# A gather, running-sum and matmul kernel: undivided gathers and stores, a shorter lead of the sums and single casts

## The chip, the cores and the metric

The kernel runs on one core of a Trainium2 chip. The metric is the device time of one execution in microseconds (us). An execution's span, from the first to the last instruction that the hardware profiler recorded, is a little shorter than its time.

## The reference

```python
B, S, N, D = (16, 4096, 2048, 512)
# x: [B, S, D] float32; indices: [B, N], sorted, without repeats; w: [D, D] float32
def reference(x, indices, w):
    b_idx = np.arange(B)[:, None]
    gathered = x[b_idx, indices, :].copy()      # 2048 rows of 2 KB for each batch
    cs = np.cumsum(gathered, axis=1)            # running sum over the gathered rows
    return np.matmul(cs, w).astype(np.float32)  # [B, N, D]
```

67.1 MB are gathered from memory and 67.1 MB are written back.

## The kernel before, in words

**Tiles.** The 16 x 2048 gathered rows are cut into T = 256 tiles of 128 rows (P = 128), 16 tiles for each batch (NT = 16). Two tiles make a pair (R = 2), so there are G = 128 pairs. Every tile goes through the same six steps, and each step is written out for one engine. There is no scheduler: every engine has its own list of instructions, and waits on semaphores (through the helper class `Lane`, whose `need` leaves out a wait already made).

1. **Gather (POOL, L138-164).** An indirect DMA fetches 128 rows of x by index into the float32 buffer `g32`, one row for each partition. There are 16 tile slots in `g32` (NG = 16, eight pairs). A pair's gathers wait until the casts of the pair that used the slots before are done (`pool.need(s_c, ...)`, L141).
2. **Cast (ACT, L169-179).** `g32` to the half-precision buffer `g16` (NH = 8 pairs). A cast waits for its gather's 16 semaphore increments, one from each DMA engine.
3. **Sums (PE, L181-196).** Four 128x128 matmuls against a triangular matrix give the running sums inside the tile, transposed, in one of four PSUM tiles `pa` (NA = 4).
4. **Carry (DVE, L198-223).** Adds the last column of the previous tile and writes `cst` (NC = 4 pairs).
5. **Product (PE, L225-240).** Four 128x512 matmuls by w into one of four PSUM tiles `pb` (NB = 4).
6. **Drain (ACT, L242-245) and store (SP, L247-267).** `pb` is copied to the output buffer `ob` (NO = 4 buffers of W = 2 pairs), and SP issues a DMA to the output: 512 KB for one pair, 1 MB for two.

**What sets the order.** On PE the list `order` (L378-386) puts the sums of tile u + LEAD ahead of the product of tile u. LEAD is 3 in the steady state; it grows from 1 at the start and shrinks to 1 at the end. On ACT the list `casts` (L125-133) says which casts stand ahead of the drain of tile u: far = 6 tiles ahead in the steady state, 2 to 5 at the start, and 5 to 3 over the last tiles. Where far is over 5 the two tiles of a pair are cast by one instruction of 128x1024; where it is smaller each tile has its own 128x512 cast. The steady states of PE, DVE and ACT are hardware loops; ACT's holds V = 3 x 16 = 48 tiles.

**Divided transfers.** Five gathers (`SPLITS`: tiles 56, 104, 152, 200 and 248) are issued in two parts. First an instruction resets the cursor of the descriptor generator (L152), then the last E = 8 partitions are gathered with an index list of their own (`idx_last`, semaphore `s_h`), and then the other 120. One store is issued in two parts as well: that of pair `ODD` = 106 and the pair after it, 1 MB, goes out as partitions 0 to 118 (`EVEN` = 119) and partitions 119 to 127 (L264-267, semaphore `s_x`).

**Stores.** The first eight pairs are stored one at a time, then two pairs per DMA, and the last two pairs one at a time (L293-298). The very first and the very last pair are stored tile by tile (L254-260).

Of the kernel before, what the change touches and what calls it, by code (L numbers as in the profile page):

```python
# [7 lines left out]
P = 128  # L8
FP32 = mybir.dt.float32
FP16 = mybir.dt.float16  # L10
U32 = mybir.dt.uint32
# [22 lines left out]
def kernel(  # L34
# [7 lines left out]
    nc = tc.nc  # L42

    B, S, D = x.shape
    N = indices.shape[1]
    R = 2
    Q = P // R
    DC = D // P
    NT = N // P
    T = B * NT  # L50
    G = T // R
    GB = NT // R
    KI = T // P
    E = 8
    EB = 3
    SPLITS = [b * NT + NT // 2 for b in range(EB, B, EB)]
    ODD = G - 11 * R
    EVEN = 119
    FIRST = 2 * R
    NG = 16  # L60
    LEAD = 3
    FAR = 6
    NH = 8
    NA = 4
    NB = 4
    NC = 4
    W = 2
    NO = 4
    U = NT
    V = EB * U  # L70
    assert U == NT == NG == W * R * NO and V % U == 0 and (T - 4 * U) % V == 0 and SPLITS[0] // V == 1 and 2 * U < SPLITS[0] and SPLITS[-1] >= T - 2 * U <= R * ODD + W * R * NO and ODD % W == 0 and U % NG == 0 and U % NA == 0 and U % (R * NC) == 0 and U % NB == 0
# [8 lines left out]
    idx_last = const.tile([E, len(SPLITS), 2], U32)  # L80
# [10 lines left out]
    g32 = [const.tile([P, R, D], FP32, name=f"g32_{i}") for i in range(NG // R)]  # L91
    g16 = [const.tile([P, R, D], FP16, name=f"g16_{i}") for i in range(NH)]
# [16 lines left out]
    s_last = sem("s_last")  # L109
    s_h = sem("s_h")  # L110
    s_f = [sem(f"s_f{i}") for i in range(NO)]
    s_x = sem("s_x")
    s_ol = sem("s_ol")
    s_g = [sem(f"s_g{i}") for i in range(NG)]
    s_o = [sem(f"s_o{i}") for i in range(NO)]
# [10 lines left out]
    cast_by = []  # L126
    for u in range(T):
        far = min(FAR, 2 if u < R else 3 + (u + 4) // 8, 3 + (T - 1 - u) // 6)
        casts.append([])
        while len(cast_by) <= min(u + far, T - 1):  # L130
            n = R if far > 5 and len(cast_by) % R == 0 else 1
            casts[u].append((len(cast_by), n))
            cast_by += [cast_by[-1] + 1 if cast_by else 1] * n

    for u in range(2 * U + U, T - 2 * U):
        assert casts[u] == [(t + U, n) for t, n in casts[u - U]]

    def gather(t):  # L138
        g, r = divmod(t, R)
        if t >= NG:  # L140
            pool.need(s_c, cast_by[R * (g + 1) - NG - 1])  # L141
        if t < FIRST:
            pool.need(s_first[g], 16)
            ap = idx_first[:, t, 0:1]
        else:
            pool.need(s_prep, t // P + 1)
            ap = idxg[:, t // P, t % P : t % P + 1]
        parts = [(0, P, ap, s_g[t % NG])]
        if t in SPLITS:

            pool.need(s_last, 16)
            nc.gpsimd.inc_swdge_sem([], [], mode="reset_dge_cursor")  # L152
            parts = [
                (P - E, P, idx_last[:, SPLITS.index(t), 0:1], s_h),
                (0, P - E, ap[: P - E], s_g[t % NG]),
            ]
        for a, b, ap, done in parts:
            nc.gpsimd.indirect_dma_start(  # L158
                out=g32[g % (NG // R)][a:b, r, :],
                out_offset=None,  # L160
                in_=x_flat,
                in_offset=bass.IndirectOffsetOnAxis(ap=ap, axis=0),
                element_offset=(t // NT) * S * D,
            ).then_inc(done, 16 * EB if done is s_h else 16)

    PLAIN = (0, 1, G - 2, G - 1)

    def cast(t, n, first=None):  # L169
        g, r = divmod(t, R)  # L170
        for u in range(t, t + n):
            act.need(s_g[u % NG], 16 * (u // NG + 1), first)
            if first is None and u in SPLITS:
                act.need(s_h, 16 * EB * (SPLITS.index(u) + 1))
            elif first is not None and u == SPLITS[0] - 2 * U:
                act.need(s_h, 16 * EB - 2 * U, first)
        nc.scalar.copy(  # L177
            out=g16[g % NH][:, r : r + n], in_=g32[g % (NG // R)][:, r : r + n]
        ).then_inc(s_c, 1)

    def sums(t, u, first=None):  # L181
        g, r = divmod(t, R)
        tiles = None if first is None else R * first
        pe.need(s_c, cast_by[t] if first is None else cast_by[2 * U + t] - 2 * U // R, first)
# [62 lines left out]
    def store(g, n):  # L247
        b, h = divmod(g, GB)
        rows = out[b, h * R * P : (h + n) * R * P, :]
        i = g // W % NO  # L250
        src = ob[i]

        done = s_ol if g >= G - W else s_f[i] if 0 < g < W * NO and g % W else s_o[i]
# [9 lines left out]
        rows = rows.rearrange(order, p=P, j=R)  # L263
        for part in (slice(0, EVEN), slice(EVEN, P)) if g == ODD else (slice(0, P),):  # L264
            nc.sync.dma_start(out=rows[part], in_=src[part, g % W : g % W + n]).then_inc(
                s_x if part.start else done, 16
            )

    with nc.allow_non_contiguous_dma(reason="a few indices, one per partition"):  # L270
        for k, eng in enumerate((nc.sync, nc.scalar)):
            t = k * R
            eng.dma_start(
                out=idx_first[:, t : t + R, :],
                in_=indices[0, t * P : (t + R) * P]
                .bitcast(U32)
                .rearrange("(t p w) -> p t w", p=P, w=2),
            ).then_inc(s_first[k], 16)
        nc.scalar.dma_start(
            out=idx_last[:],  # L280
            in_=indices[EB:B:EB, (NT // 2 + 1) * P - E : (NT // 2 + 1) * P]
            .bitcast(U32)
            .rearrange("b (p w) -> p b w", w=2),
        ).then_inc(s_last, 16)
    idx_rows = indices.bitcast(U32).rearrange("b (t q) -> (b t) q", q=2 * P)
    for k in range(KI):
        nc.sync.dma_start(
            out=idx64[:, k, :], in_=idx_rows[k * P : (k + 1) * P, :]
# [3 lines left out]
        eng.dma_start(out=w32[:, c, :], in_=w[c * P : (c + 1) * P, :]).then_inc(s_w[c], 16)  # L292
    for g in range(W * NO):  # L293
        store(g, 1)
    for g in range(W * NO, G - W, W):
        store(g, W)
    for g in range(G - W, G):
        store(g, 1)
    for i in range(G // W - NO, G // W - 1):
        sp.need(s_o[i % NO], 16 * (i // NO + 1))  # L300
    sp.need(s_ol, 16 * (R + W - 1))

    nc.gpsimd.memset(ident[:], 1.0).then_inc(s_ut, 1)
# [3 lines left out]
        out=ident[:],  # L308
        in_=ident[:],
# [7 lines left out]
        out=ut[:],  # L317
# [103 lines left out]
    def step(u, first=None):  # L421
        if u % (W * R) == 0:
            i, slot = divmod(u // (W * R), NO)
            if first is None and i == 1:
                act.need(s_f[slot], 16 * (W - 1 + (slot == 0) * (R - 1)))
            act.need(s_o[slot], 16 * i, first)
            if first is None and u == R * ODD + W * R * NO:
                act.need(s_x, 16)
        for t, n in casts[u if first is None else 2 * U + u]:
            cast(t if first is None else t - 2 * U, n, first)  # L430
        drain(u, first)

# [38 lines left out]
```

## Time and profile before

| What | Value |
|---|---|
| time, median of 9 runs | 352.31 us (351.5 to 353.89) |
| time of the profiled execution | 352.95 us |
| its span | 351.2 us |
| granted TensorE clock, mean | 0.987 |
| PE / ACT / POOL / DVE busy | 86 / 74 / 71 / 51% |
| moved by DMA | 135.69 MB, mean 386 GB/s |
| packets of the gathers' queue (q0) and of SP's queue (q1) | 50.1% and 48.0% of 16 DMA engines' span |

A line of the view of instructions by group gives: source line, engine, operation, what it writes and reads, count | busy us, mean ns of one | idle time of the engine just before, and what ended most of it. A line of the view of waits gives: who waited, for whom: us in total, times, longest. The view of a source line ends with the time from a DMA's issue to its landing, which is its last semaphore increment. In the view of stages each row gives the busy time of every engine in one stretch of the span, then the granted clock, the DMA share and GB/s. The trace also holds each transfer's 16 landing increments, one by one, with their times; it does not say which DMA engine sent which.

### The profile page before, as it was taken

The numbers are of one execution on the slowest core, as the hardware profiler recorded it, in microseconds if no ns is written. First come the engines' busy times: TensorE is split into PE (matmuls) and PEld (weight loads), VectorE is DVE, ScalarE is ACT, GpSimd is POOL, SyncE is SP. The second block draws the span as 40 slices with busy tenths as digits, with TensorE's granted clock in tenths as the row PEclk, the third lists the DMA queues.
The fourth block names the chain that finished last, engine by engine and source line by source line (L and its number), as shares of the span: only waits on it lengthen the run. The fifth ranks groups of instructions, "written<-read, shape, count | busy, mean of one in ns | idle before, by whom it ended". The sixth has DMA issues, their size and how long they took to land.

```text
span 351.2 us, 6396 instructions
## 1 busy us (share of the span) xinstructions
PE 301.5 (86%) x2066; PEld 152.2 (43%) x2066; DVE 179.2 (51%) x263; ACT 260.8 (74%) x407; POOL 248.7 (71%) x271
## 2 busy tenths in 40 slices
PE   6797969889899898988989899899898899888990
PEld 2343435434444443543544444444444444434540
DVE  1464636545555464554645555455555555544550
ACT  2686778678787877777968778778687777777980
POOL 6777777777777777777777777777777777777400
PEclk9899999999999999999999999999999999999996
DMA  6899999999999999999999999999999999999994
GB/s 201 265 323 380 384 390 343 406 408 392 403 416 413 419 419 415 404 401 412 387 406 418 418 416 410 395 416 409 418 415 389 412 407 416 338 398 412 416 381 179
DMA packets 40139, 135.69 MB, mean 386 GB/s; under 512 B 6060, under 2 KB 6316, under 8 KB 40128
## 3 DMA queue, kind: packets, MB, share of 16 engines
q0 software_dynamic: 20640, 67.13, 50.1%
q1 hardware_dynamic: 18880, 67.90, 48.0%
q10 hardware_dynamic: 608, 0.53, 0.4%
q8 instruction: 5, 0.08, 0.1%
q14 instruction: 6, 0.05, 0.0%
HBM read 68.42 MB, written 67.11 MB: 386 GB/s over the span
## 4 chain that ended last, share of the span: by engine, by line
POOL 39%; DMA 37%; issue 14%; ACT 5%; PE 2%; POOLq 0%; ACTq 0%; SPq 0%
POOL g L158 39%; DMA g<-in_x_dram,idxg 36%; ACT g L177 5%; PE pb L233 2%; ACT ob L245 1%; DMA idx_first<-in_indices_dram 1%; POOLq L338 0%; PE pa L189 0%; ACTq L26 0%; ACTq L436 0%; SPq L467 0%; SPq L98 0%
## 5 line engine op out<-in xcount | busy, mean ns | idle before, releaser
L158 POOL DMA_INDIRECT g<-in_x_dram,idxg x252 | 238.7, 947 | 76.8 <-issue 67.3
L233 PE MATMUL pb<-w,cst 128*128 128x512 f16 x1024 | 263.9, 381 | 0.7 <-DVE cst L221 0.3
L221 DVE TENSOR_TENSOR cst<-pa,cst 128x512 f16<-128x512 f32 x240 | 166.0, 692 | 140.9 <-PE pa L189 140.7
L177 ACT CAST g<-g 128x1024 f16<-128x1024 f32 (+1 forms) x147 | 137.7, 938 | 72.6 <-DMA g<-in_x_dram,idxg 71.7
L245 ACT COPY ob<-pb 128x512 f32<-128x512 f32 x256 | 138.5, 587 | 4.1 <-PE pb L233 4.1
L189 PE MATMUL pa<-ut,g 128*128 128x128 f16 x992 | 97.2, 221 | 35.9 <-ACT g L177 34.9
L189 PEld LDWEIGHTS pa<-ut,g 128*128 128x128 f16 x992 | 68.8, 98 | 116.4 <-ACT g L177 81.0
L233 PEld LDWEIGHTS pb<-w,cst 128*128 128x128 f16 x1024 | 89.6, 98 | 63.1 <-issue 1.6
L208 DVE CAST cst<-pa 128x512 f16<-128x512 f32 x16 | 11.1, 692 | 14.3 <-PE pa L189 14.3
L344 PE MATMUL pb<-zeros 128*128 128x512 f16 x16 | 5.2, 484 | 1.5 <-DVE zeros L348 1.5
L189 PE MATMUL pa<-uq,g 128*128 128x128 f16 x32 | 3.4, 232 | 2.9 <-ACT g L177 2.7
L158 POOL DMA_INDIRECT g<-in_x_dram,idx_last x5 | 4.5, 895 | 1.5 <-issue 1.5
L158 POOL DMA_INDIRECT g<-in_x_dram,idx_first x4 | 4.0, 998 | 1.6 <-issue 0.9
L189 PEld LDWEIGHTS pa<-uq,g 128*128 128x128 f16 x32 | 2.3, 103 | 5.8 <-issue 3.8
L344 PEld LDWEIGHTS pb<-zeros 128*128 128x128 f16 x16 | 1.9, 122 | 4.0 <-issue 1.9
L417 ACT ACT_TABLE_LOAD x1 | 1.3, 1283 | 3.1 <-issue 3.1
L420 ACT CAST w<-w 128x512 f16<-128x512 f32 x2 | 1.1, 614 | 3.1 <-DMA w<-in_w_dram 3.1
L351 DVE CAST idxf<-idx 128x128 f32<-128x128 uint32 x2 | 0.6, 314 | 3.6 <-DMA idx<-in_indices_dram 3.6
L365 DVE CAST w<-w 128x512 f16<-128x512 f32 x2 | 0.9, 477 | 2.4 <-DMA w<-in_w_dram 2.4
L356 PE MATMUL pb<-ident,idxf 128*128 128x128 f32 x2 | 0.6, 300 | 0.6 <-DVE idxf L351 0.6
L348 DVE MEMSET zeros<- 128x256 uint32 x1 | 0.3, 272 | 1.1 <-SPq L98 1.1
L362 DVE CAST idxg<-pb 128x128 uint32<-128x128 f32 x2 | 0.6, 288 | 0.4 <-PE pb L356 0.4
(12 smaller groups left out, 2.4 us busy)
## 6 DMA issues: line engine op xcount, KB each, us to landing
out_dram<-ob SPq DMA_DIRECT2D x58, 1024.0 KB, 8.8
out_dram<-ob SPq DMA_DIRECT2D x8, 512.0 KB, 6.4
g<-in_x_dram,idxg POOLq DMA_INDIRECT x252, 7.7
out_dram<-ob SPq DMA_DIRECT2D x4, 256.0 KB, 5.2
out_dram<-ob SPq DMA_DIRECT2D x1, 952.0 KB
w<-in_w_dram ACTq DMA_DIRECT2D x2, 256.0 KB, 4.6
w<-in_w_dram SPq DMA_DIRECT2D x2, 256.0 KB, 5.5
idx<-in_indices_dram SPq DMA_DIRECT2D x2, 128.0 KB, 2.9
```

The costliest lines, as they stand in the source:

```text
L158: nc.gpsimd.indirect_dma_start(out=g32[g % (NG // R)][a:b, r, :], out_offset=None, in_=x_flat, in_offset=bass.IndirectOffsetOnAxis(ap=ap, ...
L177: nc.scalar.copy(out=g16[g % NH][:, r : r + n], in_=g32[g % (NG // R)][:, r : r + n]).then_inc(s_c, 1)
L189: mm = nc.tensor.matmul(out=pa[t % NA][:, c], lhsT=g16[g % NH][:, r, c * P : (c + 1) * P], rhs=uq[:] if first is None and g in PLAIN else ...
L208: nc.vector.tensor_copy(out=dst, in_=src).then_inc(s_d, 1)
L221: nc.vector.tensor_tensor(out=dst, in0=src, in1=last, op=mybir.AluOpType.add).then_inc(s_d, 1)
L233: mm = nc.tensor.matmul(out=pb[u % NB][:], lhsT=cst[g % NC][:, c, j, :], rhs=w16[:, c, :], start=(c == 0), stop=(c == DC - 1),)
L245: nc.scalar.copy(out=ob[g // W % NO][:, g % W, j], in_=pb[u % NB][:]).then_inc(s_e, 1)
L344: nc.tensor.matmul(out=pb[NB - 1][:], lhsT=zeros[:, :P], rhs=zeros[:], start=True, stop=True)
L351: nc.vector.tensor_copy(out=idxf[:, k, :], in_=idx64[:, k, 0::2]).then_inc(s_if, 1)
L365: nc.vector.tensor_copy(out=w16[:, c, :], in_=w32[:, c, :]).then_inc(s_wc, 1)
L417: nc.scalar.copy(out=spare[:], in_=zeros[:, :1])
L420: nc.scalar.copy(out=w16[:, c, :], in_=w32[:, c, :]).then_inc(s_wc, 1)
```

## The change

- The five divided gathers and the one divided store become whole: `SPLITS`, `ODD`, `idx_last` with its load, the cursor resets and the semaphores `s_last`, `s_h` and `s_x` go.
- LEAD goes from 3 to 2: the sums run two tiles ahead of the products.
- FAR goes from 6 to 4, and every cast is of one tile; ACT's loop body shrinks from 48 to 16 tiles.
- The last four pairs, instead of the last two, are stored singly. The first eight stay as they were.

```diff
-    E = 8
-    EB = 3
-    SPLITS = [b * NT + NT // 2 for b in range(EB, B, EB)]
-    ODD = G - 11 * R
-    EVEN = 119
-    LEAD = 3
-    FAR = 6
+    LEAD = 2
+    FAR = 4
...
-    V = EB * U
+    V = max(U, W * R * NO)
...
     for u in range(T):
-        far = min(FAR, 2 if u < R else 3 + (u + 4) // 8, 3 + (T - 1 - u) // 6)
-        casts.append([])
-        while len(cast_by) <= min(u + far, T - 1):
-            n = R if far > 5 and len(cast_by) % R == 0 else 1
-            casts[u].append((len(cast_by), n))
-            cast_by += [cast_by[-1] + 1 if cast_by else 1] * n
+        far = 2 if u < R else 3 if u < U // 2 or T - 1 - u < R * R else FAR
+        casts.append(range(done, max(done, min(u + far + 1, T))))
+        done = max(done, min(u + far + 1, T))
...
         if t >= NG:
-            pool.need(s_c, cast_by[R * (g + 1) - NG - 1])
+            pool.need(s_c, R * (g + 1) - NG)
...
-        parts = [(0, P, ap, s_g[t % NG])]
-        if t in SPLITS:
-
-            pool.need(s_last, 16)
-            nc.gpsimd.inc_swdge_sem([], [], mode="reset_dge_cursor")
-            parts = [
-                (P - E, P, idx_last[:, SPLITS.index(t), 0:1], s_h),
-                (0, P - E, ap[: P - E], s_g[t % NG]),
-            ]
-        for a, b, ap, done in parts:
-            nc.gpsimd.indirect_dma_start(
-                out=g32[g % (NG // R)][a:b, r, :],
...
+        nc.gpsimd.indirect_dma_start(
+            out=g32[g % (NG // R)][:, r, :],
...
-    def cast(t, n, first=None):
+    def cast(t, first=None):
         g, r = divmod(t, R)
-        for u in range(t, t + n):
-            act.need(s_g[u % NG], 16 * (u // NG + 1), first)
...
+        act.need(s_g[t % NG], 16 * (t // NG + 1), first)
         nc.scalar.copy(
-            out=g16[g % NH][:, r : r + n], in_=g32[g % (NG // R)][:, r : r + n]
+            out=g16[g % NH][:, r, :], in_=g32[g % (NG // R)][:, r, :]
         ).then_inc(s_c, 1)
...
-        for part in (slice(0, EVEN), slice(EVEN, P)) if g == ODD else (slice(0, P),):
-            nc.sync.dma_start(out=rows[part], in_=src[part, g % W : g % W + n]).then_inc(
-                s_x if part.start else done, 16
-            )
+        nc.sync.dma_start(
+            out=rows.rearrange(order, p=P, j=R), in_=src[:, g % W : g % W + n]
+        ).then_inc(done, 16)
...
-    for g in range(W * NO, G - W, W):
+    for g in range(W * NO, G - 2 * W, W):
         store(g, W)
-    for g in range(G - W, G):
+    for g in range(G - 2 * W, G):
         store(g, 1)
```

More of the change, by code (lines that the diff above doesn't have):

```diff
@@ L69 @@
     U = NT
-    V = EB * U
-    assert U == NT == NG == W * R * NO and V % U == 0 and (T - 4 * U) % V == 0 and SPLITS[0] // V == 1 and 2 * U < SPLITS[0] and SPLITS[-1] >= T - 2 * U <= R * ODD + W * R * NO and ODD % W == 0 and U % NG == 0 and U % NA == 0 and U % (R * NC) == 0 and U % NB == 0
+    V = max(U, W * R * NO)
+    assert U == NT == NG == W * R * NO and V % U == 0 and V % (W * R * NO) == 0 and T % V == 0 and U % NG == 0 and U % NA == 0 and U % (R * NC) == 0 and U % NB == 0
     assert D == 512 and N % (R * P) == 0 and T % P == 0
@@ L79 @@
     idx_first = const.tile([P, FIRST, 2], U32)
-    idx_last = const.tile([E, len(SPLITS), 2], U32)
     idx64 = const.tile([P, KI, 2 * P], U32)
@@ L108 @@
     s_idx = [sem(f"s_idx{k}") for k in range(KI)]
-    s_last = sem("s_last")
-    s_h = sem("s_h")
     s_f = [sem(f"s_f{i}") for i in range(NO)]
-    s_x = sem("s_x")
     s_ol = sem("s_ol")
@@ L125 @@
     casts = []
-    cast_by = []
+    done = 0
     for u in range(T):
-        far = min(FAR, 2 if u < R else 3 + (u + 4) // 8, 3 + (T - 1 - u) // 6)
-        casts.append([])
-        while len(cast_by) <= min(u + far, T - 1):
-            n = R if far > 5 and len(cast_by) % R == 0 else 1
-            casts[u].append((len(cast_by), n))
-            cast_by += [cast_by[-1] + 1 if cast_by else 1] * n
-    for u in range(2 * U + U, T - 2 * U):
-        assert casts[u] == [(t + U, n) for t, n in casts[u - U]]
+        far = 2 if u < R else 3 if u < U // 2 or T - 1 - u < R * R else FAR
+        casts.append(range(done, max(done, min(u + far + 1, T))))
+        done = max(done, min(u + far + 1, T))
+    for u in range(2 * U, T - 2 * U):
+        assert casts[u] == range(u + FAR, u + FAR + 1)
     def gather(t):
@@ L147, in gather @@
             ap = idxg[:, t // P, t % P : t % P + 1]
-        parts = [(0, P, ap, s_g[t % NG])]
-        if t in SPLITS:
-            pool.need(s_last, 16)
-            nc.gpsimd.inc_swdge_sem([], [], mode="reset_dge_cursor")
-            parts = [
-                (P - E, P, idx_last[:, SPLITS.index(t), 0:1], s_h),
-                (0, P - E, ap[: P - E], s_g[t % NG]),
-            ]
-        for a, b, ap, done in parts:
-            nc.gpsimd.indirect_dma_start(
-                out=g32[g % (NG // R)][a:b, r, :],
[L160 to L164, printed above, removed]
+        nc.gpsimd.indirect_dma_start(
+            out=g32[g % (NG // R)][:, r, :],
+            out_offset=None,
+            in_=x_flat,
+            in_offset=bass.IndirectOffsetOnAxis(ap=ap, axis=0),
+            element_offset=(t // NT) * S * D,
+        ).then_inc(s_g[t % NG], 16)
     PLAIN = (0, 1, G - 2, G - 1)
-    def cast(t, n, first=None):
+    def cast(t, first=None):
         g, r = divmod(t, R)
-        for u in range(t, t + n):
-            act.need(s_g[u % NG], 16 * (u // NG + 1), first)
[L173 to L176, printed above, removed]
+        act.need(s_g[t % NG], 16 * (t // NG + 1), first)
         nc.scalar.copy(
-            out=g16[g % NH][:, r : r + n], in_=g32[g % (NG // R)][:, r : r + n]
+            out=g16[g % NH][:, r, :], in_=g32[g % (NG // R)][:, r, :]
         ).then_inc(s_c, 1)
@@ L183, in sums @@
         tiles = None if first is None else R * first
-        pe.need(s_c, cast_by[t] if first is None else cast_by[2 * U + t] - 2 * U // R, first)
+        pe.need(s_c, t + 1, tiles)
         pe.need(s_d, t - NA + 1, tiles)
@@ L251, in store @@
         src = ob[i]
-        done = s_ol if g >= G - W else s_f[i] if 0 < g < W * NO and g % W else s_o[i]
+        done = s_ol if g >= G - 2 * W else s_f[i] if 0 < g < W * NO and g % W else s_o[i]
         if g in (0, G - 1):
@@ L262, in store @@
         order = "(g j p) d -> p g j d" if g in PLAIN else "(g p j) d -> p g j d"
-        rows = rows.rearrange(order, p=P, j=R)
-        for part in (slice(0, EVEN), slice(EVEN, P)) if g == ODD else (slice(0, P),):
-            nc.sync.dma_start(out=rows[part], in_=src[part, g % W : g % W + n]).then_inc(
-                s_x if part.start else done, 16
-            )
+        nc.sync.dma_start(
+            out=rows.rearrange(order, p=P, j=R), in_=src[:, g % W : g % W + n]
+        ).then_inc(done, 16)
     with nc.allow_non_contiguous_dma(reason="a few indices, one per partition"):
@@ L278 @@
             ).then_inc(s_first[k], 16)
[L279 to L284, printed above, removed]
     idx_rows = indices.bitcast(U32).rearrange("b (t q) -> (b t) q", q=2 * P)
@@ L294 @@
         store(g, 1)
-    for g in range(W * NO, G - W, W):
+    for g in range(W * NO, G - 2 * W, W):
         store(g, W)
-    for g in range(G - W, G):
+    for g in range(G - 2 * W, G):
         store(g, 1)
-    for i in range(G // W - NO, G // W - 1):
+    for i in range(G // W - NO, G // W - 2):
         sp.need(s_o[i % NO], 16 * (i // NO + 1))
-    sp.need(s_ol, 16 * (R + W - 1))
+    sp.need(s_ol, 16 * (R + 2 * W - 1))
     nc.gpsimd.memset(ident[:], 1.0).then_inc(s_ut, 1)
@@ L426, in step @@
             act.need(s_o[slot], 16 * i, first)
[L427 to L430, printed above, removed]
+        for t in casts[u if first is None else 2 * U + u]:
+            cast(t if first is None else t - 2 * U, first)
         drain(u, first)
```

## The prediction

> **What bounds the kernel now.** I read four things in this order: the page's slices, the waits, POOL's own timeline, and the time that transfers take to land. In the slices the columns are 40 equal parts of the span.
>
> ```profile
> span 351.2 us, 6396 instructions
> ...
> DMA  6899999999999999999999999999999999999994
> GB/s 201 265 323 380 384 390 343 406 408 392 403 416 413 419 419 415 404 401 412 387 406 418 418 416 410 395 416 409 418 415 389 412 407 416 338 398 412 416 381 179
> ```
>
> The DMA engines are over 90% busy from the third slice to the last but one, and where nothing disturbs them they move 416 to 419 GB/s. That is 419/16 = 26.2 GB/s for one engine, so 16 KB (an engine's eighth rows of one gather) cost it 0.63 us and one 2 KB row 0.08 us. 135.69 MB at 419 GB/s are 324 us; what is above that is the start, the end and the dips. No compute engine is as full (PE 86%, in a loop of 1.09 us a tile; ACT 74%). The waits:
>
> ```profile
> ACT g L177 <- DMA g<-in_x_dram,idxg: 71.7, 94, 2.5
> POOL g L158 <- issue: 69.8, 229, 0.3
> POOL g L158 <- ACT g L177: 9.4, 31, 0.3
> ```
>
> ACT waits for gathers to land. POOL waits for nobody: its longest pause is 0.3 us, the same pause that stands ahead of each gather. So it issues one gather every 1.25 us, as its timeline shows round a divided gather:
>
> ```profile
> 72.19 0.95 POOL L158 DMA_INDIRECT g<-in_x_dram,idxg  x1 [0.30 <-issue]
> 73.44 0.90 POOL L158 DMA_INDIRECT g<-in_x_dram,idx_last  x1 [0.30 <-issue]
> 74.64 1.00 POOL L158 DMA_INDIRECT g<-in_x_dram,idxg  x1 [0.30 <-issue]
> 75.94 0.98 POOL L158 DMA_INDIRECT g<-in_x_dram,idxg  x1 [0.31 <-issue]
> ```
>
> The 8-partition piece costs POOL 1.2 us, nearly a whole gather. One tile is 256 KB in and 256 KB out: 524,288 B / 419 GB/s = 1.25 us. POOL and DMA are therefore almost equally fast, and which of them rules is told by the time from a gather's issue to its landing. For issues at 76-90, 280-295 and 312-329 us it is, in three answers one below the other (minimum, median, maximum):
>
> ```profile
> DMA to landing us min/median/max: 6.2/6.9/7.5
> ...
> DMA to landing us min/median/max: 7.9/8.2/8.7
> ...
> DMA to landing us min/median/max: 10.3/10.8/11.0
> ```
>
> Gathers 5 to 8, issued into nearly idle queues, landed in 3.7 to 4.4 us. So late gathers stand some 4 to 7 us in the DMA queues: POOL is ahead, DMA is the bound.
>
> A transfer has landed when the last of its engines has. The 16 landing increments of single gathers, read from the trace, show one engine alone behind the other fifteen: by 1.6 us for the gather issued at 20.9, 2.5 us at 68.4 (the other fifteen lie within 1.5 us of each other), 2.6 us at 293.7. A divided gather shortens that lead: 2.5 us before the one at 73.4, 1.0 us after it; 1.8 and 0.9 round the one at 134.7. After the divided store (295.3) the picture turns: seven engines are last and nine stand 3 to 6 us ahead. At the very end one engine lands the last store at 349.5, three near 347.4, twelve at 346.3.
>
> What the pieces do to single engines I take from the Trainium skill, "DMA: Bandwidth & Descriptors", section "Why a DMA increments its semaphore by 16 and not by 1": a transfer runs on the largest k up to 16 that divides its partitions; SP's use the lowest-numbered k, POOL's go on from a cursor. So 8 partitions go to engines 0-7, the other 120 to 8-15 and 0-6, and engine 7 gets 1 row instead of 8. The store's 119 go to engines 0-6 (17 each), its 9 to 0-8. That fits the seven-against-nine split above; that the laggard is number 7 the trace can't say, but the gap shrinks at the divided gathers.
>
> **The change part by part.**
>
> *POOL.* Five pieces of 0.895 + 0.30 us and five slightly longer successors: 5 x 1.25 = 6.3 us of POOL go, and the last gather is issued at 322.4 instead of 328.7. A rule speaks here for the change: the same page, "Rules for kernel authors", says not to split by partitions, to use one 128-partition transfer. By that rule and POOL's rows alone the sum would be 351.2 - 6.3 = 344.9. By the landing row it is 0: a gather issued 6.3 us earlier waits that much longer in its queue. The cover is the backlog of 4 to 7 us, and 16 slots x 1.25 = 20 us of ring. I take 0.
>
> *The laggard's load.* Each whole gather gives it back 0.63 - 0.08 = 0.55 us, five 2.7 us. The whole store gives it 64 KB instead of 8: 56 KB / 26.2 GB/s = 2.2 us. Sum +4.9 us, on an engine whose queues are not empty from about 20 us on. Engines 0-6 lose 80 KB and 5 rows, 3.5 us each. The section "Latency and other measured facts" of that page says that engines 7 and 15 are usually slower, cause unsure; it speaks against the change. The row here says one laggard, not two: with both, the last two increments would lie together.
>
> *The dip of the divided store.* The stage 294-310 us stands beside its neighbours:
>
> ```profile
> 250.00:294.00 44.00, 39.26 (x273) 19.86 (x272) 23.61 (x35) 34.30 (x52) 33.34 (x36) 1.00 1.02 408
> 294.00:310.00 16.00, 13.37 (x95) 6.92 (x96) 7.89 (x12) 11.67 (x19) 12.04 (x14) 1.00 0.99 371
> 310.00:336.00 26.00, 23.97 (x166) 12.14 (x165) 14.00 (x21) 21.09 (x37) 15.08 (x16) 1.00 1.02 410
> ```
>
> (last two columns: DMA share and GB/s.) 16 us x (409 - 371)/409 = 1.5 us of DMA are lost there, because engines run dry or crowd. This comes back; for the laggard I count half, -0.8 us (ends 0 and -1.5).
>
> *Where the laggard ended before.* Not read directly. After the divided store it was one of the nine leaders, so its work ran out between 345.5 (it keeps up with the twelve that end with the last store) and 347.6 (second-latest). Middle 346.6. After the change: 346.6 + 2.7 + 2.2 - 0.8 = 350.7, against the 349.5 at which the last engine ended: +1.2 us. Ends: 345.5 + 4.9 - 1.5 = 348.9 (-0.6) and 347.6 + 4.9 = 352.5 (+3.0).
>
> *Casts and leads.* With single casts at the start ACT runs cast and drain in 1.00 us a tile (casts at 34.80, 35.80, 36.79); a paired turn takes 1.96 us for two (53.89 after 51.93). +0.02 us a tile, under a DMA pace of over 1.25: 0, hidden by ACT's waits for landings (71.7 us); without them 256 x 0.02 = 5 us. PE with LEAD 2 has the same matmuls; its 1.09 us a tile lie under the same pace. Stores come two to three tiles sooner after landing; that puts other bytes first in full queues and wins nothing in the middle. But a landing that is late now reaches PE two to three tiles sooner, as a stall: bounds -1 (stores earlier in slices 2 to 5, which are not full) to +2 us (stalls that hold back stores and run queues dry). The start, where single casts wait up to 1.75 us without loss of pace, is the nearest row; I take +0.3, as the laggard's lateness grows.
>
> *SP, the start, the end.* One store DMA less, one more; 0.37 us each, in a queue that waits up to 6.2 us for drains: 0. The last four pairs stored singly let one 512 KB store start a pair earlier: 0 to -0.6, taken 0, since the laggard's backlog ends last. The load of `idx_last` leaves ACT's queue ahead of w; w lands (8.7) before the first gather (9.3): 0.
>
> Sum: +1.2 + 0.3 = +1.5 us on the span (352.7), as an execution 352.95 + 1.5 = 354.5. The profiled execution is 0.6 over the median of the runs, so 353.9.
>
> **Rivals.** About 0.3% (1.06 us) is what a measurement of this kernel can tell from no change.
>
> 1. *POOL was the bound after all* (faster). For it: no pause over 0.3 us, and the fifteen other engines follow POOL at a constant distance. Against: landing times grow. Place: POOL's list; price 6.3 us, of which DMA lets through only its idle time: 336-349.5 us holds some 3.6 us of unused DMA, the dip up to 1.5. So 347.5 to 350.5, decided if the laggard ended before 344. Chance 0.14.
> 2. *The laggard fills the ring.* Its lag is 2.6 + 4 x 0.55 = 4.8 us without divided gathers; with POOL 6.3 us ahead its gathers take 8.5 + 2.7 + 6.3 = 17.5 us, and a pair's slots are reissued after about 17.5 us. If the jitter on it then also starves PE and the stores, every tile goes at its pace: 355.5 to 359. For: the numbers meet. Against: only in the last quarter. Chance 0.2.
> 3. *It evens out*: the load given back lands where engines 0-6 are relieved, and both ends fall together: 351.3 to 353.3. For: the lower end of the sum. Chance 0.24.
>
> The forecast's own case, 353.4 to 355.5, has 0.42. Faster by over 0.3% (below 351.25): 0.14; within: 0.24; slower (above 353.37): 0.62. The range that leaves out 0.1 on each side: 351.0 to 357.8; the likeliest case alone: 353.4 to 355.5.
>
> **What would show each step.** Right: gathers 1.25 us apart with the last issue near 322.5 or a few POOL waits for ACT just before it; landing times of 12 to 17 us near 310; one engine alone last, by 4 to 6 us, to the end; the 338 GB/s slice gone; ACT never the releaser of PE for longer than now. Wrong: landing times flat near 8 us with POOL's end earlier (then POOL was the bound), two or more engines together last, or queues that run dry (DMA share under 0.98) in the middle.

## The result and the profile after

The changed kernel takes 348.77 us (median of 10 runs, 348.2 to 349.06). The kernel before, run beside it on the same chips, takes 352.94 us (median of 31, 351.5 to 354.08). The ratio is 0.9882 with a 95% interval of 0.9868 to 0.9896: the change makes the kernel faster by 1.2%. The prediction was 353.9 us and "slower". The profiled execution of the changed kernel took 349.1 us with a span of 347.4 us, against 352.95 and 351.2 before.

The page's slices of the changed kernel (40 equal parts of the span):

```profile
span 347.4 us, 6369 instructions
...
DMA  7899999999999999999999999999999999999974
GB/s 233 257 324 368 384 383 380 406 411 417 414 418 416 415 417 415 416 413 416 412 414 415 414 413 417 413 412 413 414 411 416 414 412 408 413 411 411 411 290 188
```

The dips are gone. Before, slices like 387, 395, 389 and 338 stood between others of up to 419. Now every slice from the ninth to the thirty-eighth lies between 408 and 418. The peaks are no higher than before; the valleys are filled. The price stands in the last slices: 411, 290, 188, where before it was 416, 381, 179.

The waits of the changed kernel (total us, times, longest us):

```profile
POOL g L136 <- issue: 67.3, 221, 0.3
ACT g L150 <- DMA g<-in_x_dram,idxg: 52.5, 158, 1.3
...
POOL g L136 <- ACT g L150: 10.4, 34, 0.3
```

ACT still waits for gathers to land, but for 52.5 us in place of 71.7, and never for longer than 1.3 us where it was 2.5. POOL still never pauses for more than 0.3 us. POOL's own timeline has its last gather here:

```profile
322.44 0.95 POOL L136 DMA_INDIRECT g<-in_x_dram,idxg  x1 [0.30 <-issue]
```

That is the 322.4 of the prediction. The time from issue to landing (minimum, median, maximum), for gathers issued at 76-90, 280-295 and 312-329 us, in three answers one below the other:

```profile
DMA to landing us min/median/max: 8.1/8.2/8.4
...
DMA to landing us min/median/max: 13.9/14.1/14.5
...
DMA to landing us min/median/max: 14.8/15.1/15.3
```

These were 6.9, 8.2 and 10.8 in the median before. So each gather waits up to 6 us longer to land, and the kernel is faster all the same. The landing increments of single gathers in the trace show where the wait lies. One engine alone is behind the median of the sixteen: by 3.2 us in the gather that has landed at 149 us, 4.8 at 211, 6.8 at 286 and 9.1 at 300 (before: 1.7 at 150, 2.6 at 286). The gap to the second-latest is 2.5, 4.6, 6.5 and 8.2 us.

Much of this is only an earlier issue. Tile 216 is gathered 5.0 us sooner than before (273.7 us, before 278.7) and has landed at 287.3 us (before 286.3). The median engine has it at 279.8 us instead of 283.7. So fifteen engines follow POOL's earlier issue, and the late one lands the same tile no sooner than before.

The stages of the changed kernel. After the window come its length, the busy time of PE, PEld, DVE, ACT and POOL (with counts), the granted clock, the DMA share and GB/s:

```profile
60.00:100.00 40.00, 37.82 (x252) 17.62 (x250) 22.15 (x32) 33.87 (x63) 30.25 (x33) 1.00 1.03 413
100.00:200.00 100.00, 93.44 (x624) 43.42 (x624) 53.54 (x78) 84.22 (x157) 75.63 (x81) 1.00 1.03 415
200.00:294.00 94.00, 87.86 (x586) 40.90 (x585) 50.60 (x74) 78.49 (x147) 71.15 (x76) 1.00 1.03 413
294.00:310.00 16.00, 14.98 (x99) 6.63 (x96) 8.63 (x13) 13.41 (x26) 12.04 (x14) 1.00 1.02 411
310.00:336.00 26.00, 24.35 (x165) 11.19 (x165) 13.84 (x20) 21.99 (x42) 10.34 (x11) 1.00 0.94 376
```

The first three of these stages in the kernel before (its last two stand in the prediction, with 371 and 410):

```profile
60.00:100.00 40.00, 34.44 (x243) 17.39 (x241) 20.76 (x30) 29.30 (x44) 30.25 (x33) 1.00 1.02 397
100.00:200.00 100.00, 90.25 (x632) 46.17 (x631) 54.49 (x79) 78.46 (x119) 75.62 (x81) 1.00 1.02 411
200.00:294.00 94.00, 84.21 (x586) 42.51 (x584) 50.67 (x74) 72.80 (x109) 71.15 (x76) 1.00 1.02 409
```

The bytes that the changed kernel is ahead can be summed from these, stage by stage, as the time that they take at the new rate. 60-100 us: 40 x 16/413 = 1.5 us. 100-200: 100 x 4/415 = 1.0. 200-294: 94 x 4/413 = 0.9. 294-310: 16 x 40/411 = 1.6. Together 5.0 us. In 310-336 us, 26 x 34/411 = 2.2 us are given back: POOL has issued everything by 322.4, fifteen engines have the last gather at 331.1 us, and the late one has it at 337.5 (DMA share 0.94). The first 60 us bring some +0.4 (271 to 284 GB/s before 30 us, 387 to 379 from 30 to 60). That makes 3.2 us by 336 us. The spans differ by 3.8; the rest of 0.6 falls after 336 us. In the stages shown the granted clock is 1.00 in both kernels. In the first 30 us it is 0.94 before and 1.00 after; a run below that also has 0.94 there (gathers and store whole) keeps most of the gain.

Bytes ahead are not yet tiles ahead. By 294 us the packet records have 0.88 MB more than before in the gathers' queue and 0.75 MB more in SP's. Four pieces fewer on POOL mean four whole gathers more by then, and these alone are 4 x 256 KB = 1.05 MB. The experiments show that the extra gathers made no tile ready sooner.

### The profile page after: what moved, and what is told of

Same layout as the page of the kernel before. It is cut to its first block, busy times and chain, and to the rows that moved or that the text cites. A ratio compares the mean times of both kernels' runs of the same rounds, so it can differ in the third digit from the quotient of the medians.

```text
span 347.4 us, 6369 instructions
## 1 busy us (share of the span) xinstructions
PE 312.8 (90%) x2066; PEld 145.8 (42%) x2066; DVE 179.2 (52%) x263; ACT 278.8 (80%) x516; POOL 244.0 (70%) x266
## 4 chain that ended last, share of the span: by engine, by line
DMA 38%; POOL 38%; issue 13%; ACT 5%; PE 2%; POOLq 0%; ACTq 0%; SPq 0%
POOL g L136 38%; DMA g<-in_x_dram,idxg 38%; ACT g L150 4%; PE pb L206 2%; ACT ob L218 2%; DMA idx_first<-in_indices_dram 1%; PE pa L162 0%; POOLq L303 0%; ACTq L26 0%; ACTq L399 0%; SPq L430 0%; SPq L92 0%
## 5 line engine op out<-in xcount | busy, mean ns | idle before, releaser
L150 ACT CAST g<-g 128x512 f16<-128x512 f32 x256 | 158.4, 619 | 55.1 <-DMA g<-in_x_dram,idxg 52.5
L218 ACT COPY ob<-pb 128x512 f32<-128x512 f32 x256 | 148.5, 581 | 2.6 <-PE pb L206 2.6
L162 PE MATMUL pa<-ut,g 128*128 128x128 f16 x992 | 98.7, 221 | 24.8 <-ACT g L150 19.3
L162 PEld LDWEIGHTS pa<-ut,g 128*128 128x128 f16 x992 | 62.9, 97 | 123.7 <-ACT g L150 109.5
```

Of the source, the lines that this page charges most:

```text
L150: nc.scalar.copy(out=g16[g % NH][:, r, :], in_=g32[g % (NG // R)][:, r, :]).then_inc(s_c, 1)
L162: mm = nc.tensor.matmul(out=pa[t % NA][:, c], lhsT=g16[g % NH][:, r, c * P : (c + 1) * P], rhs=uq[:] if first is None and g in PLAIN else ...
L218: nc.scalar.copy(out=ob[g // W % NO][:, g % W, j], in_=pb[u % NB][:]).then_inc(s_e, 1)
```

## Experiments

In some runs the kernel before took about 450 us instead of 352. The traces of the kernels run beside it have pauses of 2 to 4 us on several engines and some 300 GB/s, so other limits hold there. These runs are told apart from the rest, and every ratio is to the kernel before on the same chip in the same minutes. The condition does not go with the number of the chip: 0 and 8 stand in the record with both.

The recorded expectations speak of theories. P: POOL's pieces held the gathers back, so that the DMA queues ran dry in the middle. C: the casts in pairs and the long leads make the stores come in lumps. D: the dip of the divided store is lost on the path that sets the end.

### The changed kernel once more

No edit to the changed kernel.

> The changed kernel itself, beside the kernel before, on the chip of this call. Where the kernel before takes 352 us: 348 to 349.5 us, as on record. Where the kernel before takes 450 us (as in the runs so far, in which all engines pause for 2 to 4 us at a time, waiting on nothing that the program says): theory P expects 443 to 446 us, as the gathers made whole alone gave 443 to 445; theory C expects less than that, under 441.

Measured: 348.56 us against 353.08, ratio 0.9877 (0.9846 to 0.9909). The result repeats.

### Only the gathers whole

```diff
-    SPLITS = [b * NT + NT // 2 for b in range(EB, B, EB)]
+    SPLITS = []
```

The load of `idx_last` and the waits for `s_h` go with it; the divided store, the leads, the casts and the last stores stay as before.

> The kernel before with only the five divided gathers made whole, for a chip on which the kernel before takes 352 us. Theory P: 349.5 to 351 us, slices 12 to 33 all at 405 GB/s or more, landing times that grow past 12 us. Theory C: 352 to 354 us with slices under 400 left in the middle. My prediction's term for it: 354 to 356 us. Where the kernel before takes 450 us: 442 to 445 us again.

Measured: 353.23 us against 352.58, ratio 1.0012 (0.9998 to 1.0027): no gain, against theory P. POOL's 6.3 us are gone here too (last gather issued at 322.17), so POOL's time alone is not what the change brings. The slices of this kernel:

```profile
GB/s 232 256 324 375 360 382 379 372 415 403 414 415 415 417 415 416 415 417 414 416 415 414 413 416 415 414 413 415 412 412 416 414 412 411 341 391 412 409 307 152
```

The middle is filled just as in the changed kernel (411 to 417 from the eleventh slice to the thirty-fourth). Then the divided store stands there as the 341, and its stages:

```profile
200.00:294.00 94.00, 84.05 (x584) 42.51 (x581) 50.52 (x73) 72.71 (x110) 71.16 (x76) 1.00 1.03 414
294.00:310.00 16.00, 13.96 (x97) 6.97 (x96) 8.30 (x12) 11.91 (x19) 12.04 (x14) 1.00 0.99 363
310.00:336.00 26.00, 23.68 (x165) 12.24 (x166) 13.84 (x20) 21.33 (x38) 10.07 (x11) 1.00 0.99 398
```

The dip is deeper than before the change (363 against 371), and the stage after it is at 398 instead of 410. The gathers issued at 312-329 us land later than in any other kernel here:

```profile
DMA to landing us min/median/max: 16.2/16.6/17.2
```

In the trace the late engine is 3.3 us behind the others at the last store, which is issued at 343.3 us (343.8 before). The fuller middle is gathers that fifteen engines fetch sooner: by 294 us the gathers' queue has moved 1.20 MB more than before, and SP's queue 0.11 MB less. Tile 216 has landed at 286.8 us, 286.3 before. So no tile was ready sooner for the filled dips, and there was no gain for the divided store to take away.

### Gathers and store whole, all else as before

The edit above, and:

```diff
-        for part in (slice(0, EVEN), slice(EVEN, P)) if g == ODD else (slice(0, P),):
+        for part in (slice(0, P),):
```

> Gathers and store whole, casts and leads as before, for a chip on which the kernel before takes 352 us. If the divided store's dip and the load that its pieces put on seven engines kept e11's gain from the end: 348.5 to 350 us. If the casts and leads hold it: 351.5 to 353 us. My prediction: 354 to 356 us.

Measured: 349.74 us against 352.41, ratio 0.9924 (0.9896 to 0.9951). The two stages in which the divided store used to bite, in this kernel:

```profile
294.00:310.00 16.00, 14.56 (x103) 7.51 (x104) 8.67 (x13) 13.20 (x21) 12.04 (x14) 1.00 1.03 412
...
310.00:336.00 26.00, 24.29 (x174) 12.90 (x172) 14.44 (x22) 22.09 (x40) 10.08 (x11) 1.00 1.00 403
```

363 GB/s have become 412, that is 16 x 49/412 = 1.9 us. The last gathers, of 312-329 us, land sooner than with the divided store (16.2/16.6/17.2), though they are issued at the same times (the last at 322.2 us in both):

```profile
322.18 0.95 POOL L157 DMA_INDIRECT g<-in_x_dram,idxg  x1 [0.30 <-issue]
...
DMA to landing us min/median/max: 13.4/14.2/14.5
```

On top of whole gathers, making the store whole is worth 1.0012 - 0.9924 = 0.88%, some 3.1 us. The whole transfers together give 0.76% of the 1.2%. What the store is worth with the gathers still divided was not run on a 352-us chip. An estimate: the last gather of the kernel before is issued at 328.7 us, and if it landed after 8.2 us, as those ahead of the divided store do, or 1 us later than that, it would be in 2 to 3 us sooner than the 339.9 us of its trace. So the store alone may carry nearly all of the 0.76%, and that whole gathers are needed for it is not shown.

The ends of the kernels, from the landing increments and SP's rows of the traces (us; tile 216 lands before the divided store is issued at 295 us):

| Kernel | tile 216 landed | last gather issued | landed | last store issued | landed | span |
|---|---|---|---|---|---|---|
| before | 286.3 | 328.7 | 339.9 | 343.8 | 349.5 | 351.2 |
| gathers whole | 286.8 | 322.2 | 339.4 | 343.3 | 349.4 | 351.1 |
| gathers and store whole | 286.1 | 322.2 | 336.7 | 341.3 | 346.3 | 348.0 |
| changed | 287.3 | 322.4 | 337.5 | 341.8 | 345.7 | 347.4 |
| changed, once more | 286.6 | 322.4 | 336.8 | 341.1 | 345.0 | 346.7 |

At tile 216 no kernel is ahead. With both whole, the end comes 3.2 us sooner than before, and so does the last gather's landing. All of it arises after the divided store's place. The last store is issued 3.9 to 4.6 us after that landing in every row.

The remaining 0.45% must come from leads, single casts or last stores. In 60-100 us this kernel is at 403 GB/s and the changed one at 413, but that does not show in the table: the changed kernel's last gather lands no sooner (337.5 and 336.8 against 336.7). What is shorter there is the landing of the last store, 3.9 and 4.0 us against 5.0. Two traces of the same kernel differ by 0.7 us, so this stays a reading, not a proof.

### Relief for the late engine, late in the kernel

The changed kernel, with three gathers divided again (tiles 184, 216 and 248). For that the ACT loop ends at tile 128, and the rest of the list is written out.

```diff
+    SPLITS = [b * NT + NT // 2 for b in range(11, B, 2)]
+    LOOP_END = T // 2
...
-    with nc.scalar.Fori(2 * U, T - 2 * U, V) as first:
+    with nc.scalar.Fori(2 * U, LOOP_END, V) as first:
```

> The changed kernel with three divided gathers put back late, at tiles 184, 216 and 248, where POOL is ahead by landing times of 11 us and more (ACT's hardware loop ends at tile 128, the rest is written out, so that these casts can wait for the piece). If the late engine sets the changed kernel's end: it gets 3 x 0.55 = 1.65 us less, 347 to 348 us where the changed kernel takes 348.7, and its gap at the last gathers falls from 7-8 to 5-6 us. If the pieces only hold POOL back (3 x 1.25 us): 349 to 352 us with dips after 240 us. If the end is the chain of casts, sums, products and stores, not an engine: 348.5 to 349.

Measured: 350.12 us against 352.52, ratio 0.9933 (0.9913 to 0.9953), about 0.5% slower than the changed kernel. The late engine's gap to the second-latest, for gathers issued at 312-329 us, falls from 6.4-7.0 to 4.0-4.8 us, and they land in 12.0 us in the median, where it was 15.1. But the three pieces also cost POOL 3.7 us: the last gather is issued at 326.1 us instead of 322.4, and it has landed at 338.1, where it was 337.5 and 336.8 in the two traces of the changed kernel. So the late engine lands it no sooner, and the others lose their lead. The slices of this kernel and one of its stages:

```profile
GB/s 199 257 342 375 388 389 397 410 413 412 413 416 413 414 414 414 412 414 414 413 411 414 413 410 412 414 412 402 405 409 412 413 400 405 413 400 399 409 333 188
...
200.00:294.00 94.00, 87.53 (x584) 40.56 (x583) 50.02 (x74) 78.27 (x146) 71.14 (x76) 1.00 1.02 409
```

A slice is 8.7 us long. The pieces are issued at 233.5, 274.8 and 316.1 us, in slices 27, 32 and 37. Slices 28 and 29 (402, 405) and 33 and 34 (400, 405) follow the first two; 37 (399) holds the third, but the 400 ahead of it has no piece of its own. In 200-294 us the changed kernel is at 413. By the packet records the difference lies in the gathers' queue alone: by 294 us it has moved 0.48 MB less than in the changed kernel, about the two gathers that POOL has not issued, and SP's queue has moved as much (56.3 MB in both). The spans of the traces, 348.0 against 347.4 and 346.7 us, differ by what the last landing differs.

The control for the written-out list is this one (the changed kernel, the loop ending at tile 128, no divided gather):

> The changed kernel with ACT's loop ending at tile 128 and the rest written out, nothing else: the control for e14. If e14's loss is the pieces' own: 348.3 to 349.2 us, as the changed kernel. If it is the written-out loop: 349.7 to 350.5 us, with rates of 409 GB/s or less after 200 us.

It ran on a chip where the kernel before took 450 us: 441.33 against 453.83, ratio 0.9855 (0.978 to 0.9931), with no sign of a loss. On a 352-us chip it was not run, so the share of the written-out list in the 0.5% isn't excluded. Most of the low slices follow a piece, though, and the written-out stretch from slice 21 to 27 is at 410 to 414.

### The parts alone, where the kernel before takes 450 us

These runs were meant to share out the 1.2% and fell in the other condition. The waits of one of them (gathers and store whole, old leads; total us, times, longest us) show how different it is:

```profile
POOL g L157 <- ACT g L174: 104.5, 44, 4.0
...
PEld pb L230 <- issue: 52.1, 91, 3.2
```

POOL now waits 104.5 us for casts, where it waited 10.4 above, PE's weight loads stand still for up to 3.2 us without any wait that the profile shows, and PE is 72% of the chain that ended last. The whole span has 307 GB/s in the mean, so nothing in these runs measures the case at hand.

Gathers whole, three times:

> The kernel before with only the five divided gathers made whole; the divided store, pair casts and the leads stay. Theory P (POOL's pieces held the gathers back, so that the DMA queues ran dry in the middle): most of the gain is here, 349.5 to 351 us, and the dips under 400 GB/s between 150 and 290 us are gone. Theory C (the casts in pairs and the long leads make the stores come in lumps): no gain, 352 to 354 us, dips still there. My prediction's own term (the laggard gets 2.7 us back): 354 to 356 us.

> Again the kernel before with only the five divided gathers made whole, since the first four runs were made where the kernel before itself took 452 us and PE, not the DMA queues, ended the chain. Where the kernel before takes 352 us: theory P (POOL's pieces held the gathers back): 349.5 to 351 us, the slices between 100 and 290 us all at 405 GB/s or more. Theory C (casts in pairs and long leads): 352 to 354 us with slices under 400 left. My prediction's own term: 354 to 356 us.

> The kernel before with only the five divided gathers made whole (the edit of e1). Theory P (POOL's pieces held the gathers back, so that the DMA queues ran dry in the middle): most of the gain, 349.5 to 351 us; slices 12 to 33 all at 405 GB/s or more. Theory C (casts in pairs and long leads make the stores come in lumps): 352 to 354 us with slices under 400 left. My prediction's term for it: 354 to 356 us.

Ratios 0.9832 (0.976 to 0.9904), 0.9838 (0.9775 to 0.9901) and 0.9881 (0.9816 to 0.9946). The same edit brings 1.2 to 1.7% here and nothing where the kernel before takes 352 us.

Store whole, twice:

> The kernel before with only the divided store made whole. If the dip at 298-307 us was work lost on the path that sets the end: 350.8 to 351.8 us, seven late engines gone, end set by one engine. If the laggard decides (my prediction): 353 to 355 us. Theories P and C both: the dip of 1.5 us or less, 351 to 352.5 us.

> The kernel before with only the divided store made whole (the edit of e2). Theory D (the divided store's dip at 298-307 us is lost on the path that sets the end): 350.8 to 351.8 us. My prediction (the laggard gets 2.2 us back): 353 to 355 us. Theories P and C leave it at 352 to 353 us.

Ratios 1.0017 (0.9966 to 1.0069) and 1.0166 (1.0096 to 1.0236): nothing or a loss, not settled.

Gathers and store whole, three times:

> The kernel before with gathers and store whole, but the pair casts six ahead and the sums three ahead. Theory P: as the changed kernel but for the leads, 348.7 to 350 us. Theory C: about 351.5 to 353 us, with the middle dips still there. My prediction: 354 to 356 us.

> Gathers and store whole, pair casts and leads of before (the edit of e4). Theory P with D: 348.7 to 350 us, as the changed kernel. Theory C: 351 to 353 us, dips still there. My prediction: 354 to 356 us.

> Gathers and store whole, casts and leads as before. After e11 (gathers whole alone: 0.1% slower, the middle full, but the laggard 3.4 us late and the dip of the divided store still there): if the store's dip and the 3.5 us of extra load that its pieces put on seven engines are what kept the gain from the end, 348.5 to 350 us, and this is the whole gain. If the casts and leads hold it: 351.5 to 353 us. My prediction: 354 to 356 us.

Ratios 0.9853 (0.9797 to 0.9909), 0.9902 (0.9853 to 0.9952) and 0.9731 (0.9633 to 0.983). The last one rests on two runs.

Leads and casts alone, five times:

```diff
-    LEAD = 3
-    FAR = 6
+    LEAD = 2
+    FAR = 4
...
-            n = R if far > 5 and len(cast_by) % R == 0 else 1
-            casts[u].append((len(cast_by), n))
-            cast_by += [cast_by[-1] + 1 if cast_by else 1] * n
+            casts[u].append((len(cast_by), 1))
+            cast_by.append(len(cast_by) + 1)
```

> The kernel before with only the single casts four ahead and the sums two ahead; the divided gathers and the divided store stay. Theory C: most of the gain is here, 349.5 to 351 us, the middle at 411 to 418 GB/s, ACT's longest wait for a landing 1.3 us instead of 2.5. Theory P: 352 to 353.5 us, dips still there. My prediction: 352 to 353 us (+0.3).

> The kernel before with only single casts four ahead and sums two ahead (the edit of e3). Theory C: most of the gain, 349.5 to 351 us, the middle at 411 to 418 GB/s, ACT's longest wait for a landing about 1.3 us instead of 2.5. Theory P: 352 to 353.5 us, dips still there. My prediction: 352 to 353 us.

> The kernel before with only single casts four ahead and sums two ahead, divided gathers and store kept, for a chip on which the kernel before takes 352 us. e13 leaves 0.45% (1.6 us) of the gain to the casts, the leads and the last stores: if they bring it by themselves, 350.5 to 351.5 us, with 60-100 us at 410 GB/s or more. If they only help once POOL is ahead: 352 to 353.5 us with the dips of before. My prediction's term: +0.3, 352 to 353.

> The kernel before with only single casts four ahead and sums two ahead, once more. If they bring what e13 leaves of the gain by themselves: 350.5 to 351.5 us, with 60-100 us at 410 GB/s or more. If they only help once POOL is ahead: 352 to 353.5 us with the dips of before. My prediction's term: +0.3, 352 to 353.

> The kernel before with only single casts four ahead and sums two ahead, where the kernel before takes 352 us. If they bring what e13 leaves of the gain by themselves: 350.5 to 351.5 us, with 60-100 us at 410 GB/s or more. If they only help once POOL is ahead: 352 to 353.5 us with the dips of before. My prediction's term: +0.3, 352 to 353.

Ratios 1.0101 (1.003 to 1.0172), 1.0108 (1.007 to 1.0146), 1.0055 (0.9989 to 1.0121), 1.0103 (1.0042 to 1.0163) and 1.0159 (0.9971 to 1.0346). Two of the five intervals reach 1; the other three lie above it. In that condition shorter leads cost about 1%: an engine that pauses for 2 to 4 us uses up a lead of two tiles, at 1.25 us each, faster than one of three. That reason is argued, not shown. On a 352-us chip this part never ran alone, so its share of the gain stays open.

## Why the prediction was wrong

**The step that failed** is "*The laggard's load.*", the +4.9 us, above all its store part: "The whole store gives it 64 KB instead of 8", +2.2, which with the dip's -0.8 makes +1.4 for the whole store. On top of whole gathers the runs have -0.88% for it, some 3.1 us the other way. The prediction spread the divided store so that the late engine was spared seven eighths of its share and seven others got "3.5 us each" too much. The runs show that the late engine was not spared. With the divided store it has the last gather at 339.4 us, and without it at 336.7, from the same issue time. The second-latest engine gains more, from 334.9 to 330.3 us. So the divided store delayed both, the late engine by 2.7 us where a relief of 2.2 was put down. This is what one would see if the late engine were one of the seven; the trace does not say which engine is which, so the cause stays open.

The gathers' part, +2.7, did not arrive either. Four of the five divided gathers lie ahead of tile 216, for which the step has 4 x 0.55 = 2.2 us. That tile landed at 286.3 us before, 286.8 with the gathers whole, and 286.1 with gathers and store whole. The lag behind the median did grow, but because the median moved ahead by 3.9 to 5.2 us. The gap that the step was read from is also unsteady before the change: 2.5 us for the gather issued at 68.4 us, 0.1 to 1.9 for those of 76-90.

**POOL, "I take 0",** holds for the gathers alone. Before, the last one is issued here:

```profile
328.69 0.95 POOL L158 DMA_INDIRECT g<-in_x_dram,idxg  x1 [0.30 <-issue]
```

With the gathers alone made whole it is issued 6.5 us sooner and has landed 0.5 us sooner (339.4 against 339.9 us), at a ratio of 1.0012. Whether POOL's time is worth something once the store is whole needs the run that is missing. The cover was misread, though: "the backlog of 4 to 7 us" is that of the latest engine. Half of the engines had the gathers of 280-295 us 5.8 us after issue (median over these gathers), where half have a gather in nearly empty queues after 3.3 to 3.4 us; so most engines had some 2.4 us of cover. That did no harm to the sum, because a tile waits for the latest engine.

**Where the end went.** The forecast had the late engine end at 350.7 us. In the changed kernel the last gather has landed at 337.5 us, 6.5 us after the second-latest engine had it, and the last store is issued at 341.8. The last two stores of the kernel before:

```profile
L257 SPq DMA_DIRECT2D out_dram<-ob x2: 351/351/351, 342.7 to 343.8; - x2
...
DMA to landing us min/median/max: 3.6/4.7/5.8
```

and of the changed kernel:

```profile
L230 SPq DMA_DIRECT2D out_dram<-ob x2: 332/332/332, 340.7 to 341.8; - x2
...
DMA to landing us min/median/max: 3.3/3.6/3.9
```

The last store is issued 2.0 us sooner and lands in at most 3.9 us instead of 5.8, so the last landing falls at 345.7 us. Together that is about the 3.8 us between the spans. The late engine still sets when the last tile is ready: the fifteen others had that gather at 331.1 us.

**The dip of the divided store, -0.8 us (ends 0 and -1.5),** was right in kind and too small. It is 16 x 40/411 = 1.6 us between the two kernels, past the far end. What the divided store leaves behind it was not in the term: in the run with whole gathers the stage after it is at 398 GB/s, with the whole store at 403, and the late engine is 3.3 us behind at the last store.

**Casts and leads, +0.3 us (bounds -1 to +2).** The sign is open on a 352-us chip. What is not explained by whole transfers is -0.45%, some 1.6 us, and these edits and the last stores share it. It lies past the lower bound. No stall came: ACT's waits for landings became shorter (1.3 us at the longest), although landings took longer from their issue, so the feared "landing that is late now reaches PE sooner" did not occur.

**SP, the start and `idx_last`, 0.** In bytes the first 60 us brought some 0.4 us; whether any of it reached the end is not shown.

**The rivals.** The measured time lies in the stretch of the first rival, 347.5 to 350.5. Its range was hit by luck. Its reason, "POOL was the bound after all", is not what the runs show: fifteen engines did follow POOL, but POOL's 6.3 us alone gave 1.0012, and the gain came with the whole store. The second rival, that the lag fills the ring, fell: POOL waited for casts no longer than before, 0.3 us at a time, because landings stopped at 15.3 us, short of the 17.5 us that it needed. The third, that it evens out, has in its range what the gathers alone did; relief of the seven engines, which it named, is what the whole store brought, and the late engine's end did not rise against it.

**The signs** that the prediction listed as "right" all came: gathers to 322.44 us, landings of 14.8 to 15.3 us, one engine last by 6.4 to 7.0 us in them (4 to 6 was listed), the 338 gone. They came while the time went the other way. They tested where the load lies, not what it costs. No sign asked whether the late engine lands the same tile later than before, and that would have told: tile 216 and the last gather in the table above.

**What stays open.** Why the divided store delays the late engine too; the whole store with the gathers still divided, and leads, casts and the last stores each alone, on a 352-us chip; and why the same kernel takes 450 us in some runs. No kernel of the study was faster than the changed one.

## What to carry to other kernels

A landing time is the time of the slowest of sixteen engines. When a change issues transfers sooner, a longer landing time and a fuller middle say little: compare when the last engine lands the same tile before and after. Here tile 216 landed within 1.0 us of before in every kernel of the table, while the rates of the middle rose. An uneven transfer in full queues is dear: a 1 MB store of 119 + 9 partitions cost 3.1 us on top of whole gathers, and it delayed the engine that it was thought to spare. When a part alone gives nothing, the other part must be run alone too before the gain is called joint; here that run is missing.

## What the runs showed of the hardware that was not expected

- A rate can rise by 4 GB/s over 200 us with no tile ready sooner: with whole gathers alone 415 and 414 GB/s in place of 411 and 409, by gathers that fifteen engines had sooner, while tile 216 landed at 286.8 us in place of 286.3. A 4 KB packet of a gather took 161.0 ns in the mean at 100-200 us, where it was 164.0 before; the cause stays open.
- In full queues the late engine is late in gathers only: for gathers issued at 280-312 us it is 6.3 to 8.5 us behind the second-latest, while the last engine of a store that lands at 285-333 us is 0.1 to 0.6 us behind. In the last stores of the kernel one engine is last again, by 1.6 us in the changed kernel and 3.3 us with the divided store. The Trainium skill, "DMA: Bandwidth & Descriptors", section "Latency and other measured facts", calls two engines usually slower and ties that, as a best guess, to transfers whose descriptors POOL makes. The trace agrees with the tie in the full queues and has one engine, not two; it does not show the cause.
- The same page's "Rules for kernel authors" advises one 128-partition transfer in place of divided ones. The runs put a number on it here: 0.76% for five gathers and one store. The gathers alone gave nothing (1.0012); the 1 MB store of 119 + 9 partitions, standing in full queues, gave 0.88% on top of them.
- A kernel can take 450 us in some runs and 352 in others, and the same edit can change its worth with it: whole gathers 0.983 to 0.988 there, 1.001 here.
